# A decoder trunk on one core: the second pair of delta rule heads starts beside the first, two attention heads change places with it, and the embedding results are written from ScalarE

## The chip, the cores and the metric

The kernel runs on one core of a Trainium2 chip. Its time is the device time of one execution in microseconds (us). A core has a matrix engine, TensorE (PE in the rows), and VectorE (DVE), ScalarE (ACT), GpSimd (POOL) and SyncE (SP); each of them works through its own list of instructions strictly in the order in which they were written, and waits where an operand is not there yet. DMA transfers are issued from the queues of SP, POOL or ScalarE.

## The reference

A trunk of two residual layers over 512 positions of width 1024. Layer 0 (even) has two groups of heads that read one input projection: four gated delta rule heads (here a0 to a3, keys and values 128 wide) and four differential attention heads (b0 to b3, two softmax maps of width 64 each). Layer 1 (odd) has eight forgetting attention heads. Each layer ends with a squared-ReLU MLP and with a per-layer embedding that is projected to width 1024 and gated. All of it is float32.

```
# a delta rule head: chunks of 64 positions, then a scan over 8 chunks
kk  = einsum(kb, k) * decay;  a_mat = strict_lower(kk) + eye
sol = triangular_solve(a_mat, [v * beta, kb * exp(gc)])
v_new = u - w @ S;   o = q_dec @ S + qk @ v_new;   S = S * g_last + k_dec^T @ v_new
# a differential head: blocks of 128 queries
a = softmax(mask(q1 k1^T)) - lam * softmax(mask(q2 k2^T));   o = a @ v
# per layer: x += sigmoid(W h) * (p[i] @ w_ple_proj)
```

## The kernel before

Every large matrix is held as a sum of a high and a low part, so that a product takes three matmuls. In the even layer TensorE has two kinds of work. The **fill** is the large projections, which depend on nothing but weights that SP's queue loads into `raw` buffers and ScalarE (`whl`, high part) and VectorE (`whl`, low part) split. The **chains** are the heads: long sequences of short steps, in each of which TensorE waits for another engine.

`even_mixer` is a planner. Its last loop keeps a modelled time, `PE.time`; a chain that is due is moved on by one step, and otherwise the next 128x512 product of the fill is written. The fill comes in the order of one string,

```
ORDER = "a0 a1 w0 v0 v1 b0 b1 a2 a3 w2 b2 b3"
```

where a*h* is the q and k projection of delta head h (48 products of 128x512), w0 and w2 are the values of two delta heads (48 products), v0 and v1 are the values of the differential heads (96 products of 128x256 each), and b*h* is the q and k projection of differential head h (48). Behind the string follow z0 and z1, the output gates of the delta heads, and two passes of `p_proj`: eight transposes of the embedding in a `raw` buffer, two high and low splits of them, then 48 products, whose results ScalarE copies into `pj` and a DMA writes to `p_out` (L343, from SP's queue). A job is written as soon as its condition holds (z0: two delta heads and two differential heads done; z1: all delta heads and three differential heads done; b*h*: head h-2 done). A scheduler afterwards orders the instructions of each engine by when it takes them to be ready.

A delta head (`gdn_head`) runs in two halves. The first, from q and k, makes the decays `et`, the scaled keys `kd`, and with the other head of its pair (0 and 1, 2 and 3) a tile of small triangles. These `small_inverses` copies out to DRAM (`lsc`) and back, broadcast over partitions into `lb` (eight DMAs of POOL's queue, L465); then POOL solves them in 15 dependent steps of a product into `xt` and an addition to `xc` (L471, L473), and builds `x` from them (L560). The second half transposes `x` into `z`, doubles the inverse level by level (`ub`, `yy`), and runs the scan over the chunks (`state`, `vn`, `u`); at its end `rs_t` or `ro` is a reciprocal root on POOL. Heads 2 and 3 begin only when heads 0 and 1 are done (the first line of `gdn_head`, with `ABREAST = 2`).

A differential head (`diff_head`) needs its q and k rotated (`rot`, L727), split into maps in `hl` buffers; then for each block of 128 queries: scores on TensorE (`ax<-hl` and `ax<-kl,hl`), the row maximum on VectorE, the exponential `p` on ScalarE (L920), transposes of `p`, the copy `at` (L937) and the product with the values. Head h begins when head h-1 has begun its last blocks (`started`, at block 1).

The `hl` buffers form one ring of eight tiles. It holds the values of the differential heads (two, all the time), the maps of a head (two), the splits of the embedding (two) and the finished heads (one each).

Of the kernel before, what the change touches and what calls it, by code (L numbers as in the profile page):

```python
# [18 lines left out]
P = 128  # L19
# [49 lines left out]
LAT_A, LAT_B = 1.55, 1.7  # L69
W_G, W_B, W_T, W_V, W_Q = 10.0, 22.5, 20.0, 6.0, 3.6  # L70
Z_B, DSTEP = 3, 3.47
ORDER = "a0 a1 w0 v0 v1 b0 b1 a2 a3 w2 b2 b3"
ABREAST = 2
N_SP = 10
N_ST = 5
SRAW, SWHL, SA = 8, 3, 4
ORDER_MID, ORDER_END = (1, 5, 6, 7, 3, 4, 2), (1, 2, 5, 6, 3, 7, 4)
# [20 lines left out]
def trunk(ctx: ExitStack, tc: tile.TileContext, I, cst, out):  # L98
# [40 lines left out]
    def v3(ap):  # L139
        return ap.rearrange("p (i c) -> p i c", c=P)  # L140
# [182 lines left out]
    def p_proj(layer, stage):  # L323

        pr = tile_of(rawp, F32, "raw")[:, 0:1024].rearrange("p (i c) -> p i c", c=256)
        nc.sync.dma_start(pr, I["p"][layer, 0].rearrange("(i p) c -> p i c", p=P))
        pT = []
        for kt in range(2):
            ps = acc()
            for i in range(NT):  # L330
                PE.transpose(ps[:, i * P:(i + 1) * P], pr[:, i, kt * P:(kt + 1) * P], ident)
            t = hl()
            split(*t, ps)
            pT.append(t)
        yield
        for c in range(2):
            w = wide(I["w_ple_proj"][layer], 0, 512 * c, rawp, whp)
            for i in range(NT):
                ps = acc()
                tok_steps(ps, pT, w, i, slice(0, 512), (0, 1), True, True)  # L340
                y = stage("pj")
                S.activation(out=y, in_=ps, func=AF.Copy)
                nc.sync.dma_start(p_out[layer][i * P:(i + 1) * P, 512 * c:512 * c + 512], y)  # L343
                yield


    def even_mixer(act, first, wba):
        w_in = I["w_in_even"][0]
        with ExitStack() as es:
# [108 lines left out]
            def small_inverses(pair):  # L458

                lc, n = small_l[pair], 2 * NT  # L460
                lsc = dp.tile([P // BASE, BASE * n * BASE], F32, tag="lsc", name="lsc", bufs=1)
                G.dma_start(lsc.rearrange("b (r n) -> b r n", r=BASE), lc.rearrange("p h i c -> p (h i c)"))
                lb = gp.tile([P, BASE, n, BASE], F32, tag="lb", name="lb", bufs=1)
                for a in range(P // BASE):
                    G.dma_start(lb[a * BASE:(a + 1) * BASE].rearrange("p r i c -> p (r i c)"),  # L465
                                lsc[a:a + 1, :].broadcast_to([BASE, BASE * n * BASE]))
                yield 10.0
                xc = small_w[pair].rearrange("p h i c -> p (h i) c")
                tmp = gp.tile([P, n, BASE], F32, tag="xt", name="xt", bufs=1)
                for c in range(BASE - 1, 0, -1):  # L470
                    G.tensor_tensor(out=tmp[:, :, 0:c], in0=lb[:, c, :, 0:c],  # L471
                                      in1=xc[:, :, c].broadcast_to([P, n, c]), op=ALU.mult)
                    G.tensor_tensor(out=xc[:, :, 0:c], in0=xc[:, :, 0:c], in1=tmp[:, :, 0:c], op=ALU.add)  # L473
                yield 10.0
                solved.append(pair)

            def gdn_head(h, qT, kT):
                while len(done) < h + 1 - ABREAST or h >= ABREAST and h not in vts:
                    yield 2.0
                if h >= ABREAST:  # L480
                    yield from decays(h)
                blk = [slice(i * P, (i + 1) * P) for i in range(NT)]
# [5 lines left out]
                pk = aux()  # L488
                for i in range(NT):
                    PE.transpose(pk[:, blk[i]], kT[:, blk[i]], ident)  # L490
                sq, kk = st_("sqk"), gp.tile([P, 2, NT], F32, tag="kk", name="kk", bufs=ABREAST)
                for i in range(NT):
                    S.activation(out=sq[:, blk[i]], in_=pk[:, blk[i]], func=AF.Square, accum_out=kk[:, 0, i:i + 1])
                kd = sp("kd")
                S.activation(out=kd, in_=pk, func=AF.Copy)
                dg = st_("dg")
                V.tensor_tensor(out=v3(dg), in0=v3(pg), in1=mid(gm["minus_base"]), op=ALU.mult)
                second = pair in small_l
# [34 lines left out]
                for i in range(NT):  # L533
                    PE.matmul(pq[:, blk[i]], lhsT=kT[:, blk[i]], rhs=qT[:, blk[i]], start=True, stop=True)
                V.tensor_tensor(out=et, in0=pq, in1=et, op=ALU.mult)
                G.tensor_tensor(out=v3(kd), in0=v3(kd), in1=bc(hcol("ekd", h)), op=ALU.mult)

                pq = aux()
                for i in range(NT):
# [13 lines left out]
                V.tensor_tensor(out=v3(vb), in0=v3(pv), in1=bc(n2), op=ALU.mult)  # L553
                yield 2.0

                while pair not in solved:
                    yield 1.0
                x, xc = sp("x"), small_w[pair][:, sub]
                for i in range(NT):
                    G.tensor_tensor(out=x[:, blk[i]].rearrange("p (b c) -> p b c", c=BASE),  # L560
# [128 lines left out]
            def project_a(h):  # L689
# [11 lines left out]
                    if h < ABREAST:  # L701
                        silu(tiles[-1])
                heads_a.append(tiles[0])
                late.extend(tiles if h >= ABREAST else [])
                spawn(gdn_head(h, *tiles), W_G)

            def values_a(h):
                w = wload(w_in, [(C_V + h * P, 2 * P)])
                for m in range(2):
                    ps = acc()  # L710
                    yield from gemm_steps(ps, w, m, act)
                    late.append(conv_tile(ps, 8 + h + m, "vT"))
                silu(*late)
                for m in range(2):
                    vts[h + m] = late[m - 2], PE.time + W_V * LAT_A
                late.clear()

            def project_b(h):
                c = h * P
# [185 lines left out]
    def diff_head(h, qk, vt, lam, gp, heads, started, done, spawn):  # L905
# [43 lines left out]
        for i in range(NT):  # L949
            yield from values(i, pr[i])  # L950
            if i + 2 < NT:
                pr.append(probs(i + 2))
            if i == 1:
                started.append(h)
            yield DSTEP
        spawn(diff_norm(h, o, gp, heads, done), 1.5, LAT_B)
# [544 lines left out]
```

## Time and profile before

| | us |
|---|---|
| median of 3 runs | 1409.69 (1409.29 to 1410.71) |
| profiled execution | 1409.46, its span 1407.7 |
| TensorE busy | 1379.1 (98%) |
| even layer's mixer, 80 to 325 | 245.0, of it TensorE busy 233.6 |

The mean clock granted to TensorE over the span was 0.995 of full speed. The profile's stretches give for each engine its busy time and the clock; a stretch in which TensorE is neither idle nor below clock 1.00 has nothing to give. The view of waits says for whom TensorE stood still, and the chain of waits goes back from there to the instruction that started late.

### The profile page before, as it was taken

To read this page: it belongs to the slowest core of one execution; us is meant where nothing else is said; L and a number is where in the kernel's file an instruction comes from. 1 tells how busy PE (TensorE), PEld (TensorE's weight loads), DVE (VectorE), ACT (ScalarE), POOL (GpSimd) and SP (SyncE) were. 2 spreads that over 40 slices of the span, in tenths; PEclk is the share of its full clock that TensorE was granted. 3 is DMA by queue.
4 is the path that set the end of the run, shared out by engine and by line. 5 is a ranking of instruction groups with operands and counts; after the bars stand their busy time and mean duration, and the time that the engine had idled before them with its cause. 6 is when DMAs were issued, how large, how long until landed. Compare 5 with 4: busy or idle time off the path is not lost.

```text
span 1407.7 us, 18582 instructions
## 1 busy us (share of the span) xinstructions
PE 1379.1 (98%) x6969; PEld 1146.6 (81%) x6969; DVE 868.3 (62%) x1543; ACT 770.9 (55%) x1302; POOL 178.5 (13%) x241
## 2 busy tenths in 40 slices
PE   8999998999999999999999999999999999999997
PEld 6887876777888888888788888888888888888787
DVE  6847775665555566556856747556646565566675
ACT  6757775764455455554644535535455556455553
POOL 1361054200110110101001000000011020110100
PEclk9999999999999999999999999999999999999999
DMA  6361126126575665748342543661485475765711
GB/s 181 79 116 39 59 80 147 60 87 213 159 172 149 158 155 148 165 136 211 83 97 46 69 95 62 67 84 61 134 245 128 151 168 148 164 148 152 184 54 61
DMA packets 137470, 173.00 MB, mean 123 GB/s; under 512 B 10034, under 2 KB 91524, under 8 KB 137124
## 3 DMA queue, kind: packets, MB, share of 16 engines
q1 hardware_dynamic: 118480, 133.25, 34.9%
q0 software_dynamic: 15936, 35.79, 14.8%
q10 hardware_dynamic: 2964, 2.77, 0.7%
q8 instruction: 55, 0.90, 0.3%
q14 instruction: 35, 0.29, 0.1%
HBM read 156.97 MB, written 6.42 MB: 116 GB/s over the span
## 4 chain that ended last, share of the span: by engine, by line
PE 87%; DVE 5%; ACT 3%; issue 2%; DMA 1%; POOL 1%; POOLq 0%; SPq 0%; ACTq 0%; DVEq 0%
PE mm L90 57%; PE ax L90 26%; PE ax L94 3%; DMA sraw<-w_mlp_down 1%; DVE whl L149 1%; DMA raw<-w_in_even 1%; ACT rot L727 0%; DVE sa L149 0%; DVE swhl L149 0%; DVE x_tok L321 0%; ACT whl L146 0%; ACT L435 0%; POOL rs_t L259 0%; POOL ro L673 0%; ACT swhl L146 0%
## 5 line engine op out<-in xcount | busy, mean ns | idle before, releaser
L90 PE MATMUL mm<-act,whl 128*128 128x512 f32 (+1 forms) x2784 | 653.6, 387 | 0.7 <-ACT act L146 0.5
L90 PEld LDWEIGHTS mm<-act,whl 128*128 128x128 f32 x2784 | 503.1, 188 | 98.9 <-ACT act L146 1.0
L90 PE MATMUL ax<-swhl,sa 128*128 128x512 f32 x1344 | 315.1, 390 | 1.7 <-DVE sa L149 1.6
L90 PEld LDWEIGHTS ax<-swhl,sa 128*128 128x128 f32 x1344 | 251.3, 188 | 56.7 <-DVE sa L149 3.3
L149 DVE TENSOR_TENSOR whl<-raw,whl 128x1024 fp32r<-128x1024 f32 (+1 forms) x139 | 170.5, 1228 | 178.8 <-ACT whl L146 175.3
L149 DVE TENSOR_TENSOR swhl<-sraw,swhl 128x1024 fp32r<-128x1024 f32 x112 | 136.8, 1222 | 119.7 <-ACT swhl L146 119.7
L146 ACT ACTIVATE whl<-raw 128x1024 fp32r<-128x1024 f32 x140 | 148.0, 1057 | 58.4 <-PE mm L90 48.0
L146 ACT ACTIVATE swhl<-sraw 128x1024 fp32r<-128x1024 f32 x112 | 118.7, 1060 | 99.0 <-PE ax L90 80.8
L90 PE MATMUL mm<-whl,act 128*128 128x256 f32 (+2 forms) x720 | 107.3, 306 | 0.2 <-ACT act L146 0.2
L1287 ACT ACTIVATE r<-mm 128x512 f32<-128x512 f32 x64 | 38.2, 596 | 122.7 <-PE mm L90 122.7
L90 PEld LDWEIGHTS mm<-whl,act 128*128 128x128 f32 x720 | 97.3, 190 | 6.6 <-ACT act L146 0.5
L1191 POOL DMA_DIRECT2D sraw<-w_mlp_down x48 | 57.6, 1219 | 250.0 <-DVE swhl L149 103.4
L321 DVE TENSOR_TENSOR x_tok<-x_tok,ax 128x512 f32<-128x512 f32 x114 | 73.7, 681 | 5.6 <-PE ax L90 5.6
L90 PE MATMUL mm<-owhl,act 128*128 128x256 f32 (+1 forms) x336 | 57.9, 329 | 0.0
L90 PE MATMUL mm<-whl,hl 128*128 128x512 f32 x204 | 55.2, 406 | 0.9 <-DVE hl L149 0.8
L90 PE MATMUL mm<-owhl,hl 128*128 128x512 f32 x228 | 54.8, 396 | 0.0
L90 PEld LDWEIGHTS mm<-owhl,act 128*128 128x128 f32 x336 | 49.6, 188 | 6.3
L314 POOL TENSOR_TENSOR rn<-tn,nhalf 128x1 f32<-128x1 f32 x12 | 6.6, 553 | 377.2 <-DVE tn L313 377.2
L1191 POOL DMA_DIRECT2D sraw<-sraw x16 | 14.5, 906 | 300.5 <-DVE swhl L149 275.7
L90 PEld LDWEIGHTS mm<-owhl,hl 128*128 128x128 f32 x228 | 42.4, 188 | 10.1
L1200 ACT ACTIVATE sraw<-sraw 128x1024 f32<-128x1024 f32 x32 | 33.8, 1057 | 26.6 <-DVE swhl L149 15.4
L146 ACT ACTIVATE act<-ax 128x512 fp32r<-128x512 f32 x40 | 22.6, 594 | 43.9 <-PE ax L94 43.9
(341 smaller groups left out, 1596.9 us busy)
## 6 DMA issues: line engine op xcount, KB each, us to landing
raw<-w_mlp_up SPq DMA_DIRECT2D x64, 512.0 KB, 4.2
sraw<-w_mlp_down SPq DMA_DIRECT2D x64, 512.0 KB, 4.5
sraw<-w_mlp_down POOLq DMA_DIRECT2D x48, 512.0 KB, 5.9
raw<-w_in_even SPq DMA_DIRECT2D x32, 256.0 KB, 3.7
sraw<-sraw POOLq DMA_DIRECT2D x16, 512.0 KB, 6.6
raw<-w_ple_gate SPq DMA_DIRECT2D x16, 512.0 KB, 4.5
raw<-w_in_odd SPq DMA_DIRECT2D x16, 512.0 KB, 6.0
raw<-w_in_odd SPq DMA_DIRECT2D x32, 256.0 KB, 6.5
```

The costliest lines, as they stand in the source:

```text
L90: return self.tc.nc.tensor.matmul(out, lhsT=lhsT, rhs=rhs, start=start, stop=stop, skip_group_check=onto)
L94: return self.tc.nc.tensor.transpose(out, in_, ident)
L146: S.activation(out=hi, in_=src, func=AF.Copy)
L149: return (E or V).tensor_tensor(out=lo, in0=src, in1=hi.bitcast(F32), op=ALU.subtract)
L314: G.tensor_tensor(out=r, in0=t, in1=nhalf[:, 0:1], op=ALU.pow)
L321: V.tensor_tensor(out=x_tok[i][:, cs], in0=x_tok[i][:, cs], in1=ps, op=op)
L1191: G.dma_start(o, t, accum_op=ALU.add)
L1200: S.activation(out=t, in_=t, func=AF.Copy, scale=-1.0)
L1287: S.activation(out=r, in_=ps, func=AF.Relu)
```

## The change

The order of the fill is different, heads 2 and 3 no longer wait for heads 0 and 1 before their first half but before `x` is built, and with that some buffers change: `kd` of heads 2 and 3 is made late, from a second transposition of the keys, by one VectorE multiplication in place of a copy on ScalarE and a multiplication on POOL; the triangles come back into two `hl` tiles, by 16 DMAs of half the size, rows 8 to 15 of each triangle first. The heads b1 to b3 may begin at block 0 of the head before, and the results of the embedding products are written from ScalarE's queue.

```diff
-ORDER = "a0 a1 w0 v0 v1 b0 b1 a2 a3 w2 b2 b3"
+ORDER = "a0 a1 w0 v0 b0 a2 a3 b1 w2 v1 b2 b3"
-N_SP = 10
+N_SP = 14
 ...
-                nc.sync.dma_start(p_out[layer][i * P:(i + 1) * P, 512 * c:512 * c + 512], y)
+                nc.scalar.dma_start(p_out[layer][i * P:(i + 1) * P, 512 * c:512 * c + 512], y)
 ...
-                lb = gp.tile([P, BASE, n, BASE], F32, tag="lb", name="lb", bufs=1)
-                for a in range(P // BASE):
-                    G.dma_start(lb[a * BASE:(a + 1) * BASE].rearrange("p r i c -> p (r i c)"),
-                                lsc[a:a + 1, :].broadcast_to([BASE, BASE * n * BASE]))
+                lbs = [hl32().rearrange("p a (r i c) -> p (a r) i c", r=BASE // 4, c=BASE) for _ in range(2)]
+                part = BASE // 2 * n * BASE
+                for j in (1, 0):
+                    for a in range(P // BASE):
+                        G.dma_start(lbs[j][a * BASE:(a + 1) * BASE].rearrange("p r i c -> p (r i c)"),
+                                    lsc[a:a + 1, j * part:(j + 1) * part].broadcast_to([BASE, part]))
 ...
             def gdn_head(h, qT, kT):
-                while len(done) < h + 1 - ABREAST or h >= ABREAST and h not in vts:
-                    yield 2.0
 ...
-                kd = sp("kd")
-                S.activation(out=kd, in_=pk, func=AF.Copy)
+                if h < ABREAST:
+                    kd = sp("kd")
+                    S.activation(out=kd, in_=pk, func=AF.Copy)
 ...
-                while pair not in solved:
+                while pair not in solved or len(done) < h + 1 - ABREAST:
                     yield 1.0
+                if h >= ABREAST:
+                    kd, pk = sp("kd"), aux()
+                    for i in range(NT):
+                        PE.transpose(pk[:, blk[i]], kT[:, blk[i]], ident)
+                    V.tensor_tensor(out=v3(kd), in0=v3(pk), in1=bc(hcol("ekd", h)), op=ALU.mult)
 ...
-                late.extend(tiles if h >= ABREAST else [])
-                spawn(gdn_head(h, *tiles), W_G)
+                if h < ABREAST:
+                    spawn(gdn_head(h, *tiles), W_G)
+                else:
+                    late.append(tiles)
+                if h == HA - 1:
+                    silu(*(t for pair in late for t in pair))
+                    for j, pair in enumerate(late):
+                        spawn(gdn_head(ABREAST + j, *pair), W_G)
 ...
-            if i == 1:
+            if i == 0:
                 started.append(h)
```

Three places of the written order show what that moves. The first is TensorE where the first differential head begins. Before, the values of all heads (`mm<-whl,act`, of v0 and v1) and then b0's 48 and some of b1's products stand ahead of b0's scores (`ax<-hl`):

```order
L90 MATMUL mm<-whl,act 128x256 x42
L94 MATMUL ax<-gen,rope_w 128x128 x8
L90 MATMUL mm<-whl,act 128x256 x66
L90 MATMUL mm<-act,whl 128x512 x79
L90 MATMUL ax_1173<-hl 128x256
L90 MATMUL ax_1173<-kl,hl 128x256
L90 MATMUL mm<-act,whl 128x512
```

In the changed kernel v1 is gone from here, and the products of a2 and a3 stand behind b0's:

```order
L90 MATMUL mm<-whl,act 128x256 x12
L90 MATMUL mm<-act,whl 128x512 x15
L94 MATMUL ax<-gen,rope_w 128x128 x8
L90 MATMUL mm<-act,whl 128x512 x83
L94 MATMUL ax<-gen,x 128x128 x3
L90 MATMUL mm<-act,whl 128x512 x15
L90 MATMUL ax_1089<-hl 128x256
L90 MATMUL ax_1089<-kl,hl 128x256
```

The scores of b0 now come behind 113 products of 128x512, of which the first 48 are b0's own (before 79), and the first transposes of `x` of a delta head, which stood behind these scores, stand ahead of them.

The second place is POOL at the triangles of heads 2 and 3. `ub` of the level doubling and `rs_t` belong to the heads ahead or beside. Before:

```order
L462 DMA lsc<-lc 128x128
L259 TENSOR_TENSOR rs_t<-rs_t,nhalf 128x4
L465 DMA lb<-lsc 16x2048 x8
L583 TENSOR_TENSOR ub<-u,gmask 128x512 x2
L588 TENSOR_TENSOR ub<-u,gmask 128x4x32 x2
L471 TENSOR_TENSOR xt<-lb,xc 128x8x15
L473 TENSOR_TENSOR xc<-xc,xt 128x8x15
```

In the changed kernel the loads go into two tiles of the ring, and the root `ro` of a finished head of the first pair stands ahead of the first solving step:

```order
L462 DMA lsc<-lc 128x128
L467 DMA hl_1746<-lsc 16x1024 x8
L467 DMA hl_1745<-lsc 16x1024 x8
L680 TENSOR_TENSOR ro<-sso,nhalf 128x4
L473 TENSOR_TENSOR xt<-hl_1746,xc 128x8x15
L475 TENSOR_TENSOR xc<-xc,xt 128x8x15
L473 TENSOR_TENSOR xt<-hl_1746,xc 128x8x14
```

The solving of the second pair thus follows the end of a head of the first pair on POOL's list.

The third place is TensorE in the last steps of the differential heads. Before, embedding or gate products (`mm<-whl,hl`) stand between one block's scores and the next:

```order
L90 MATMUL mm<-whl,hl 128x512 x2
L90 MATMUL ax_3004<-hl,at 128x128
L90 MATMUL ax_3007<-hl 128x384
L90 MATMUL ax_3007<-kl,hl 128x384
L90 MATMUL ax_3018<-hl 128x384
L90 MATMUL ax_3018<-kl,hl 128x384
L90 MATMUL mm<-whl,hl 128x512 x2
L94 MATMUL ax_3032<-gen,p_2756 128x128 x4
L90 MATMUL mm<-whl,hl 128x512 x10
```

In the changed kernel:

```order
L90 MATMUL ax_3172<-hl,at 128x128
L90 MATMUL ax_3175<-hl 128x384
L90 MATMUL ax_3175<-kl,hl 128x384
L90 MATMUL ax_3186<-hl 128x384
L90 MATMUL ax_3186<-kl,hl 128x384
L94 MATMUL ax_3259<-gen,p_3032 128x128 x2
L90 MATMUL ax_3264<-hl,at 128x128 x2
L90 MATMUL ax_3268<-hl 128x512
L90 MATMUL ax_3268<-kl,hl 128x512
L90 MATMUL ax_3279<-hl 128x512
L90 MATMUL ax_3279<-kl,hl 128x512
L90 MATMUL mm<-whl,hl 128x512 x48
```

The last two blocks of b3 stand there without any fill between them, and the 48 products of the second embedding pass come behind its last scores.

## Rows read from the trace of the kernel before

**Rows 1.** the page: busy time, share of the span and instructions of each engine

```profile
PE 1379.1 (98%) x6969; PEld 1146.6 (81%) x6969; DVE 868.3 (62%) x1543; ACT 770.9 (55%) x1302; POOL 178.5 (13%) x241
```

**Rows 2.** stretches of the even layer: length, busy by engine, clock, DMA, GB/s

```profile
80.00:120.00 40.00, 38.89 (x212) 32.56 (x211) 22.12 (x46) 24.41 (x44) 19.57 (x40) 0.96 0.45 90
...
160.00:200.00 40.00, 38.25 (x221) 31.60 (x220) 29.81 (x70) 32.85 (x79) 12.60 (x12) 1.00 0.27 83
200.00:240.00 40.00, 34.09 (x154) 25.91 (x153) 25.80 (x61) 23.20 (x57) 16.13 (x26) 0.91 0.58 134
...
280.00:325.00 45.00, 42.59 (x241) 33.80 (x240) 30.80 (x78) 27.57 (x70) 4.45 (x4) 1.00 0.28 92
```

**Rows 3.** PE's waits, 20 to 340: us in total, times, longest

```profile
PE mm L94 <- ACT pj L342: 5.3, 1, 5.3
PE ax L90 <- DVE hl L745: 1.6, 2, 1.1
```

**Rows 4.** a stretch of 2 us inside 200 to 240, columns as rows 2

```profile
226.00:228.00 2.00, 2.00 (x6) 1.22 (x7) 0.39 (x3) 0.00 (x0) 1.08 (x1) 0.50 0.98 252
```

**Rows 5.** chain of waits, 209 to 232: start, us, what

```profile
213.37 7.45 DMA raw<-w_in_even
...
220.90 1.06 ACT whl L146
```

**Rows 6.** POOL in time order, first pair: start, us, count, idle before

```profile
74.22 3.92 POOL L465 DMA_DIRECT2D lb<-lsc  x8
87.90 0.41 POOL L471 TENSOR_TENSOR xt<-lb,xc 128x120 f32<-128x120 f32 x1 [9.77 <-DMA lb<-lsc]
...
104.49 4.46 POOL L560 TENSOR_TENSOR x<-xc,gmask 128x128 f32<-128x128 f32 x8
```

**Rows 7.** POOL in time order, second pair

```profile
176.74 1.03 POOL L673 TENSOR_TENSOR ro<-sso,nhalf 128x4 f32<-128x4 f32 x1 [59.68 <-DVE sso L672]
...
226.92 1.27 POOL L583 TENSOR_TENSOR ub<-u,gmask 128x512 f32<-128x512 f32 x1 [2.58 <-DMA p_out<-pj]
...
235.68 0.41 POOL L471 TENSOR_TENSOR xt<-lb,xc 128x120 f32<-128x120 f32 x1
...
250.96 3.83 POOL L560 TENSOR_TENSOR x<-xc,gmask 128x128 f32<-128x128 f32 x8
```

**Rows 8.** PE in time order: start, us, product, tile, count

```profile
28.28 15.28 PE L90 MATMUL mm<-act,whl 128*128 128x512 f32 x66
...
72.74 5.28 PE L90 MATMUL mm<-whl,act 128*128 128x256 f32 x42
77.86 1.04 PE L94 MATMUL ax<-gen,rope_w 128*128 128x128 f32 x8
...
173.41 0.39 PE L90 MATMUL ax<-state,qT 128*128 128x128 f32 x2
```

**Rows 9.** chain of waits behind b0's k projection, 97 to 107

```profile
98.19 0.59 ACT rot L727
...
101.91 1.18 DVE whl L149
...
104.42 0.68 DVE kl L149
...
105.85 0.67 PE ax L90 x2
```

**Rows 10.** ScalarE by line, 20 to 330: count, busy us, mean ns, idle before

```profile
L920 ACT ACTIVATE p<-ax,mx 128x128 f32<-128x128 f32 (+3 forms) x32 | 16.8, 526 | 8.1 <-DVE mx L917 7.3 <-PE ax L94 0.4
...
L937 ACT ACTIVATE at<-ax 128x128 f32<-128x128 f32 (+3 forms) x16 | 7.0, 440 | 4.1 <-PE ax L94 3.7
L920 ACT ACTIVATION_READ_ACCUMULATOR p<-ax,mx 128x1 f32 x32 | 6.3, 197 | 0.0
```

**Rows 11.** ScalarE in time order around a Silu of the gate

```profile
306.77 1.28 ACT L758 ACT_TABLE_LOAD   x1
308.07 0.60 ACT L758 ACTIVATE zt<-mm 128x512 f32<-128x512 f32 x1
```

More of the change, by code (lines that the diff above doesn't have):

```diff
@@ L470, in small_inverses @@
                 for c in range(BASE - 1, 0, -1):
-                    G.tensor_tensor(out=tmp[:, :, 0:c], in0=lb[:, c, :, 0:c],
+                    G.tensor_tensor(out=tmp[:, :, 0:c], in0=lbs[c // 8][:, c % 8, :, 0:c],
                                       in1=xc[:, :, c].broadcast_to([P, n, c]), op=ALU.mult)
@@ L490, in gdn_head @@
                     PE.transpose(pk[:, blk[i]], kT[:, blk[i]], ident)
-                sq, kk = st_("sqk"), gp.tile([P, 2, NT], F32, tag="kk", name="kk", bufs=ABREAST)
+                sq, kk = st_("sqk"), gp.tile([P, 2, NT], F32, tag="kk", name="kk", bufs=HA)
                 for i in range(NT):
                     S.activation(out=sq[:, blk[i]], in_=pk[:, blk[i]], func=AF.Square, accum_out=kk[:, 0, i:i + 1])
-                kd = sp("kd")
-                S.activation(out=kd, in_=pk, func=AF.Copy)
+                if h < ABREAST:
+                    kd = sp("kd")
+                    S.activation(out=kd, in_=pk, func=AF.Copy)
                 dg = st_("dg")
@@ L535, in gdn_head @@
                 V.tensor_tensor(out=et, in0=pq, in1=et, op=ALU.mult)
-                G.tensor_tensor(out=v3(kd), in0=v3(kd), in1=bc(hcol("ekd", h)), op=ALU.mult)
+                if h < ABREAST:
+                    G.tensor_tensor(out=v3(kd), in0=v3(kd), in1=bc(hcol("ekd", h)), op=ALU.mult)
                 pq = aux()
@@ L703, in project_a @@
                 heads_a.append(tiles[0])
-                late.extend(tiles if h >= ABREAST else [])
-                spawn(gdn_head(h, *tiles), W_G)
+                if h < ABREAST:
+                    spawn(gdn_head(h, *tiles), W_G)
[5 more added lines that the diff above has]
+                        spawn(gdn_head(ABREAST + j, *pair), W_G)
             def values_a(h):
                 w = wload(w_in, [(C_V + h * P, 2 * P)])
+                tiles = []
                 for m in range(2):
@@ L711, in values_a @@
                     yield from gemm_steps(ps, w, m, act)
-                    late.append(conv_tile(ps, 8 + h + m, "vT"))
-                silu(*late)
+                    tiles.append(conv_tile(ps, 8 + h + m, "vT"))
+                silu(*tiles)
                 for m in range(2):
-                    vts[h + m] = late[m - 2], PE.time + W_V * LAT_A
-                late.clear()
+                    vts[h + m] = tiles[m], PE.time + W_V * LAT_A
             def project_b(h):
```

## The prediction

> **What bounds the kernel now.** I read the page first: TensorE is busy for 98% of the span [rows 1], so a gain can only be idle time of TensorE, lost clock, or work taken off it. The stretches show where the even layer has any [rows 2]. Four of them matter here: 80 to 120 has 1.1 us idle and a clock of 0.96, 160 to 200 has 1.75 us idle at full clock, 200 to 240 has 5.9 us idle at 0.91, and 280 to 325 has 2.4 us idle at full clock. A clock of 0.96 over 40 us costs 1.6 us, one of 0.91 costs 3.6 us. Inside 200 to 240 a row of 2 us shows 0.50, the lower of the two levels (1.2 GHz), while TensorE is busy throughout; it follows the long wait [rows 4].
>
> The waits then say for whom TensorE stood [rows 3]: 5.3 us in one piece for `pj`, which frees the accumulator that the transposes of the embedding need, and 1.6 us for b0's rotated maps. The first of these names ScalarE's copy, but the chain of waits goes further back: a load of weights took 7.45 us to come in, and only then could ScalarE do the split for which it stood, with the `pj` copy behind it [rows 5]. The load ran while POOL's eight triangle broadcasts of the second pair were under way, as the DMA column of the same time (0.58 against 0.27 to 0.45 in the other three) lets one expect [rows 2].
>
> **The change part by part.** All fill keeps its amount; a 128x512 product costs 15.28 / 66 = 0.2315 us, a 128x256 one 5.28 / 42 = 0.126 us [rows 8].
>
> Gains. (a) b0's wait goes: 65 products of other heads, 15 us, now lie between its k projection and its scores, where 31 lay, 7.2 us. The chain there takes 105.85 - 98.19 = 7.7 us [rows 9], so 1.1 us of wait and the 1.6 us of clock go. (b) In 200 to 240 the triangles' solving and the embedding products no longer meet: the second pair's triangles are now copied ahead of v1, far ahead of the embedding products, so that the late load loses its neighbour. 5.9 + 3.6 = 9.5 us. (c) v1's 96 products now fill the end of the first pair's scan, 1.75 us idle in 160 to 200. Sum 14.0 us. The 2.4 us of 280 to 325 I leave standing: b3's end is still there.
>
> That `p_out` is written from ScalarE I cost at nothing. TensorE's wait for `pj` came from a load that arrived late, not from the issue of the write, so the queue does not touch its cause [rows 3, 5]. The Trainium skill, in "Trainium Kernel Development and Optimization" (Key Constraints), says that DMAs from all queues run on the same 16 engines and that issuing from several engines saves only the time of issue; by that the move is worth nothing either, and no row here shows the move itself. If ScalarE's issues are not hidden, 16 of them stand behind copies in a queue that is busy 58% of 200 to 240 [rows 2]; the most that they could add is within (L4) below.
>
> Costs. (L0) Heads 2 and 3 transpose their keys again: eight more transposes on TensorE. Eight of them took 1.04 us [rows 8]: 1.0 us. The `kd` work moves from ScalarE and POOL to VectorE, of which each has room.
>
> (L1) First pair's `x`. From 72.74, the start of the 128x256 run, TensorE has 12 of these (1.5), 15 + 83 products of 128x512 (22.7) and eight transposes (0.8) ahead of the transposes of `x`: it is there at 97.7. POOL issues 16 DMAs from 74.22, at 3.92 / 8 = 0.49 us each until 82.1, then solves in 104.49 - 87.90 = 16.6 us and builds three blocks of `x` in 3 x 4.46 / 8 = 1.7 us [rows 6]: 100.4. The wait is 2.7 us. It is 1.2 us if the solving takes the 250.96 - 235.68 = 15.3 us of the second pair [rows 7], and 8.5 us if the triangles land as late as before (start at 87.90). I take 2.7. Behind this wait stand the scores of b0, but no fill can pass.
>
> (L2) Second pair's `x`. POOL's list has the root `ro` of a finished first head ahead of the first solving step, and a chain from TensorE's last `state,qT` product to that root took 176.74 - 173.41 = 3.3 us [rows 7, 8]. Then come `ro` 1.0, the solving 15.3 with, in between, a second root, `rs_t` and three `ub` (1.0, 1.0, 2.5, 0.9), and half of `x`, 1.9: 26.9 us. TensorE meanwhile has 39 products of 128x256 (4.9), 40 of 128x512 (9.3), four scores (1.7) and some 43 small ones (about 4.5): 20.4 us. The wait is 6.5 us; 7.8 with the first pair's 16.6; 1.1 if the five foreign instructions find their time in gaps. I take 6.5, since POOL's list is strict.
>
> (L3) Between b2's k projection and b2's first scores TensorE has only eight transposes of the embedding, eight of `z`, eight small products and two of the embedding, about 3.0 us. The chain of b0 took 7.7 us there, 1.2 of it a weight's split [rows 9]; without that 6.5, and its durations alone, four rotations at 0.59 and four operations of VectorE and ScalarE at 0.6 to 0.7, make 5.0. So 3.5, from 2.0 to 4.7.
>
> (L4) The end of b3. The ring of eight is full there: values 2, maps of b3 2, finished b0 and b1 2, gated a-heads 2. The splits of the second embedding pass have to wait until b3's last scores free the maps, and so its 48 products, all the fill that is left, stand behind them. From b3's second block to its third, ScalarE has two exponentials with their accumulators at 0.53 + 0.20 [rows 10], two loads of the activation table at 1.28 and a Silu between at 0.60 [rows 11], `at` copies, one of 0.60 and the others at 0.3 to 0.44 [rows 10], a weight split at 1.06 [rows 5] and some smaller: 8.9 us, against 6.1 us of TensorE work. That is 2.8 us of wait. After it comes a serial piece: `at` 0.44, an exponential 0.72, two splits 0.63 each, one remainder 0.68: 3.1 us. Together 6.0. The lower end is the serial piece, 3.1; the upper end adds the two other table loads of this stretch, 8.5.
>
> (L5) Clock. A wait like that of 200 to 240 cost 3.6 us of clock behind it, a short one 1.6 [rows 2]. One of the large kind, 3.6, is what I take, from 0 to both and a second large one, 8.4 (rounded down from 8.8).
>
> Sum: 1.0 + 2.7 + 6.5 + 3.5 + 6.0 + 3.6 = 23.3; less 14.0: **+9.3 us**. The profiled execution took 1409.5 (1.8 more than its span), the median is 1409.7, so they stand for each other: 1418.8 us.
>
> **The rivals.** *The late load again.* The triangles, now 16 smaller DMAs, meet another weight load; ScalarE, strict in its order, stands again, and the 9.5 us of (b) are not had: 1418.8 + 9.5 = 1428.3 us. For it: 7.45 us for one load beside eight DMAs [rows 5]. Against it: it took one such meeting out of two, and the first pair's triangles cost no wait on TensorE.
>
> *The written order fits.* The scheduler put each of TensorE's instructions where it expects the operand; if the chains keep that pace, all four waits come out at their low ends at once: 1.0 + 1.2 + 1.1 + 2.0 + 3.1 + 0 - 14.0 = -5.6, that is 1403.9 us. It decides where L1 to L5 together stay below 10.2 us, for then the kernel is faster by over 2.8. For it: before, the same scheduling left TensorE 98% busy, and most of what it lost has one DMA as its root [rows 1, 5]. Against it: b0's 1.6 us shows that a chain can be later than the order expects [rows 3], and POOL and the ring bind whatever it expects.
>
> *Between them.* If only L2 and the clock come out low (1.1 and 0), the sum is 1.0 + 2.7 + 1.1 + 3.5 + 6.0 - 14.0 = +0.3: 1409.8 us, no change.
>
> *Dearer table loads.* In the trace a load of the table takes 1.28 us, and the Silu starts 0.02 us behind it [rows 11]. If a load in the crowded end also made ScalarE empty its queue first, for about as long as the load itself, three of them would make L4 3.8 us longer: 1422.6 us. Against it stands that row. "ScalarE: Activation LUTs" of the Trainium skill (What ACT_TABLE_LOAD costs) has such a drain, of about 1.38 us beside a load of 1.28; by that figure it would be 4.1 us and an estimate of 1422.9.
>
> **How the numbers follow.** What one measurement of this kernel can tell from no change is 0.2%, 2.8 us. My forecast has a chance of 0.47, the late load 0.10, dearer tables 0.05; these three are slower, 0.62 together. The order that fits has 0.28, faster. The case between has 0.10. The forecast's own range, with two of its terms at an end, is 1412 to 1427. The whole range reaches down to the faster case, 1403, and up past the late load, to 1431; all costs at their upper ends would give 1.0 + 8.5 + 7.8 + 4.7 + 8.5 + 8.4 - 14.0 = +24.9, which I leave out.
>
> **What would show it.** In the changed profile, waits of TensorE for `x` at two places (for the first pair around 98, for the second 100 us later), for `hl` of b2, and for `p` or `at` in b3's last blocks, each of 2 to 7 us; TensorE's list without the wait for `pj` of 5.3 us; full clock in 80 to 120. The forecast is wrong if the even layer ends earlier than before: then either POOL starts its second solving well ahead of TensorE (no wait for `x`), or the split of the embedding comes into the ring before b3 ends. A `raw` load of over 7 us with ScalarE waiting for it would speak for the late load.

## The result and the profile after

The changed kernel takes 1431.74 us (1428.67 to 1432.89, 5 runs) against 1409.29 for the kernel before (1408.00 to 1410.71, 5 runs): 1.0155 times as long, interval 1.0144 to 1.0166. The direction was forecast, but +9.3 us and at most 1431 were too little for +22.4. The profiled execution has a span of 1429.9 us, 22.2 more than before, and all of it is in the even layer's mixer: the second half of its output projection (`mm<-owhl,hl`) begins at 355.74, before at 333.55.

The page of the changed kernel, engine line: eight matmul instructions more than in [rows 1], and 10 us more busy time.

```profile
PE 1389.4 (97%) x6977; PEld 1155.5 (81%) x6977; DVE 871.9 (61%) x1545; ACT 767.5 (54%) x1296; POOL 180.1 (13%) x255
```

The four stretches of [rows 2] in the changed kernel (third column TensorE busy, then the other engines; the third figure from the end is the clock):

```profile
80.00:120.00 40.00, 34.77 (x135) 26.56 (x133) 19.82 (x37) 19.10 (x32) 17.05 (x44) 0.87 0.35 85
160.00:200.00 40.00, 39.94 (x268) 35.21 (x268) 28.93 (x89) 23.97 (x71) 17.26 (x31) 1.00 0.28 82
200.00:240.00 40.00, 32.70 (x213) 26.58 (x212) 28.47 (x59) 23.81 (x51) 19.13 (x38) 0.88 0.19 54
280.00:325.00 45.00, 38.12 (x156) 28.52 (x157) 26.08 (x73) 28.41 (x62) 4.17 (x3) 0.81 0.26 88
```

Only 160 to 200 got better. The waits of TensorE between 20 and 360 us (total, times, longest) replace those of [rows 3], of which none is left (the name behind the arrow is the last thing that the profile saw TensorE wait for):

```profile
PE ax L90 <- ACT at L950: 6.8, 4, 4.8
PE mm L90 <- DVE qT L429: 3.2, 1, 3.2
PE ax L94 <- DVE mx L930: 3.0, 1, 3.0
PE mm L90 <- ACT hl L146: 2.4, 1, 2.4
PE mm L90 <- ACT whl L146: 1.5, 1, 1.5
...
PE ax L90 <- ACT x L630: 1.1, 1, 1.1
```

Behind the longer of them the clock falls to its lower level (1.2 GHz). Stretches of 2 us, columns as above:

```profile
88.00:90.00 2.00, 2.00 (x7) 1.54 (x6) 0.00 (x0) 0.00 (x0) 1.69 (x5) 0.50 0.00 0
92.00:94.00 2.00, 2.00 (x10) 1.66 (x9) 0.00 (x0) 0.93 (x1) 1.61 (x6) 1.00 0.00 0
236.00:238.00 2.00, 2.00 (x6) 1.33 (x7) 1.17 (x5) 0.00 (x0) 0.00 (x0) 0.50 0.33 115
...
306.00:308.00 2.00, 1.35 (x5) 1.14 (x5) 1.28 (x8) 1.04 (x4) 0.88 (x1) 0.50 0.00 0
312.00:314.00 2.00, 2.00 (x6) 1.53 (x5) 1.97 (x5) 0.60 (x1) 0.00 (x0) 0.50 0.00 0
316.00:318.00 2.00, 2.00 (x11) 1.63 (x10) 0.65 (x2) 1.88 (x5) 0.00 (x0) 1.00 0.36 133
```

At 88 and at 312 TensorE is never idle and still does 6 or 7 products where it does 10 or 11 at 92 and 316. So a wait can cost twice: its own length, and the slow stretch behind it. In TensorE's time order (start, us, products, in brackets the idle time) the end of b3 shows both, the waits at 299 to 307 and the fill, which begins only behind the last scores:

```profile
293.59 0.60 PE L94 MATMUL ax<-gen,p 128*128 128x128 f32 x4
299.03 2.08 PE L90 MATMUL ax<-hl,at 128*128 128x128 f32 x8 [4.84 <-ACT at L950]
...
301.75 0.79 PE L90 MATMUL ax<-hl,at 128*128 128x128 f32 x2 [0.43 <-ACT at L950]
...
306.65 1.22 PE L90 MATMUL ax<-hl,at 128*128 128x128 f32 x4 [1.32 <-ACT at L950]
...
310.43 13.60 PE L90 MATMUL mm<-whl,hl 128*128 128x512 f32 x48
```

For all runs I made the same account, from windows of 2 us between 20 us and the start of `mm<-owhl,hl`. Idle is length minus TensorE's busy time; slowed is the sum of (1 - clock) times busy time; the rest is the start of `mm<-owhl,hl` less both. One profiled execution each; the medians are of all timed runs. Where the profiled execution lay off its median (e2 3.6 us above it, e18 2.4 above, e10 3.1 below, e11 2.0 below), the account is that of this execution.

| run | median | `owhl` starts | idle | slowed | rest |
|---|---|---|---|---|---|
| before | 1409.3 | 333.6 | 13.4 | 4.8 | 315.4 |
| changed | 1431.7 | 355.7 | 24.4 | 16.4 | 314.9 |
| e1_pout_sync | 1431.6 | 355.3 | 25.0 | 14.0 | 316.4 |
| e2_zb2 | 1429.3 | 355.3 | 22.5 | 16.6 | 316.2 |
| e3_wt18 | 1415.9 | 339.1 | 17.5 | 5.0 | 316.6 |
| e4_spin | 1430.9 | 356.2 | 18.9 | 9.2 | 328.0 |
| e5_spin2 | 1429.0 | 352.4 | 20.8 | 11.1 | 320.5 |
| e6_order_on_before | 1416.5 | 339.8 | 16.7 | 6.1 | 317.0 |
| e7_old_order | 1441.7 | 366.1 | 23.9 | 24.9 | 317.3 |
| e8_wt18_solve_dve | 1415.7 | 337.7 | 14.4 | 3.0 | 320.2 |
| e9_spin_all | 1428.8 | 353.4 | 17.6 | 8.0 | 327.8 |
| e10_started_on_before | 1427.8 | 347.7 | 17.3 | 14.7 | 315.7 |
| e11_pout_on_before | 1407.1 | 329.0 | 12.1 | 0.0 | 316.9 |
| e12_early_pair_on_before | 1425.2 | 348.8 | 24.3 | 8.4 | 316.1 |
| e13_pt_outside_ring | 1428.5 | 350.2 | 22.4 | 10.9 | 316.9 |
| e14_pt_and_solve | 1423.3 | 345.2 | 21.1 | 4.9 | 319.2 |
| e15_early_pair_pt_outside | 1414.0 | 336.9 | 15.9 | 3.3 | 317.7 |
| e16_before_pout_pt | 1407.4 | 332.6 | 12.5 | 2.9 | 317.1 |
| e17_pt_and_exp_gate | 1427.6 | 346.5 | 22.6 | 7.8 | 316.1 |
| e18_before_pout_exp_gate | 1410.4 | 335.3 | 12.2 | 6.6 | 316.5 |

The rest is 315 to 318 us in most runs, 320 to 328 with added products (e4, e5, e9), and 319 and 320 in e14 and e8, which solve the second pair's triangles on VectorE; why these two are higher was not traced. From before to after it did not grow, so idle and slowed time hold the whole change: idle grew by 11.0 us and slowed by 11.6. How it divides between the two is known to some 2 or 3 us only: e1, which takes as long as the changed kernel, has 25.0 and 14.0.

### The profile page after: what moved, and what is told of

It is laid out like the page before. It is cut to its first block, busy times and chain, and to the rows that moved or that the text cites. A ratio compares the mean times of both kernels' runs of the same rounds, so it can differ in the third digit from the quotient of the medians.

```text
span 1429.9 us, 18591 instructions
## 1 busy us (share of the span) xinstructions
PE 1389.4 (97%) x6977; PEld 1155.5 (81%) x6977; DVE 871.9 (61%) x1545; ACT 767.5 (54%) x1296; POOL 180.1 (13%) x255
## 4 chain that ended last, share of the span: by engine, by line
PE 88%; DVE 4%; ACT 3%; POOL 1%; issue 1%; DMA 1%; POOLq 0%; ACTq 0%
PE mm L90 59%; PE ax L90 26%; PE ax L94 3%; DMA sraw<-w_mlp_down 1%; ACT rot L740 0%; DVE whl L149 0%; ACT hl L146 0%; DVE swhl L149 0%; DVE sa L149 0%; POOL x L567 0%; DVE x_tok L321 0%; ACT swhl L146 0%; POOL xc L475 0%; POOL xt L473 0%; ACT whl L146 0%
## 5 line engine op out<-in xcount | busy, mean ns | idle before, releaser
L90 PE MATMUL mm<-whl,act 128*128 128x256 f32 (+2 forms) x720 | 110.4, 308 | 0.2 <-ACT act L146 0.2
L90 PEld LDWEIGHTS mm<-whl,hl 128*128 128x128 f32 x204 | 40.5, 203 | 11.6 <-ACT hl L146 3.0
L1213 ACT ACTIVATE sraw<-sraw 128x1024 f32<-128x1024 f32 x32 | 33.8, 1057 | 24.9 <-DVE swhl L149 15.3
```

The costliest lines, as they stand in the source:

```text
L90: return self.tc.nc.tensor.matmul(out, lhsT=lhsT, rhs=rhs, start=start, stop=stop, skip_group_check=onto)
L1213: S.activation(out=t, in_=t, func=AF.Copy, scale=-1.0)
```

## The experiments

All are compared with runs of the kernel before on the same chip (medians 1408.56 to 1409.84). Each edit also lets the scheduler order the engines' lists anew, so a difference is that of the edit with its new order.

**Which part of the change costs.** Each part alone, on the kernel before or with the old order.

```diff
 # e6_order_on_before: the kernel before with
+ORDER = "a0 a1 w0 v0 b0 a2 a3 b1 w2 v1 b2 b3"
 # e10_started_on_before: the kernel before with
-            if i == 1:
+            if i == 0:
 # e11_pout_on_before: the kernel before with
-                nc.sync.dma_start(p_out[layer]...
+                nc.scalar.dma_start(p_out[layer]...
 # e7_old_order: the changed kernel with
+ORDER = "a0 a1 w0 v0 v1 b0 b1 a2 a3 w2 b2 b3"
 # e12_early_pair_on_before: e7_old_order with
+            if i == 1:
 # e1_pout_sync: the changed kernel with nc.sync.dma_start(p_out[layer]...
```

e6_order_on_before: 

> The kernel before with the new order of the fill alone; heads 2 and 3 still begin when heads 0 and 1 are done. Theory (the order of the fill takes the cover from the places where TensorE then waits): slower than before by 6 to 25 us, 1416 to 1435 us, with waits in the stretch behind 280 us and half clock there. Rival (the early first half of heads 2 and 3 on POOL and the triangles in the ring make the loss, not the order): within 3 us of before, 1407 to 1413 us.

e7_old_order: 

> The changed kernel with the old order of the fill; all its other parts stay. Theory: b3's last blocks have fill between them again and keep full clock, most of the 22 us go: 1408 to 1416 us. Rival (POOL's list, in which the roots of the first pair and the solving of the second stand in each other's way, makes the loss): 1422 us or more.

e10_started_on_before: 

> The kernel before with one part of the change alone: a differential head may begin at block 0 of the head before. Theory (with the old order and the late second pair there is fill between the blocks): within 4 us of before, 1406 to 1414 us. Rival (the heads b that overlap more are what uses the fill up before the end): slower by 6 us or more, 1416 us and above.

e12_early_pair_on_before: 

> The changed kernel with the old order of the fill and with the old start of the differential heads: of the change the early first half of heads 2 and 3 is left, with its buffers, and the queue of the embedding results. Theory (the early first half is the part that with the old order costs 32 us, since its small steps use the fill's cover early and the triangles fill POOL's list and the ring): 1430 to 1445 us. Rival (the differential heads that overlap more make the most of it): 1410 to 1420 us.

The order alone costs 6.7 us (1416.53 against 1409.84; ratio 1.0034 to 1.0064), the early second pair on the old order, with its buffers and ScalarE's queue, 16.5 us (1425.20 against 1408.70; 1.0097 to 1.0131), between its theory and its rival, the earlier start of the b heads 19.1 us (1427.83; 1.0114 to 1.0148), and both of the latter with the old order 31.9 us (1441.74 against 1409.84; 1.0212 to 1.0242). So in e7 and e10 the theory failed, and in e6 its size held but its place was wrong (a wait of 6.4 us for `x`, and not one behind 280). With the new order the start of the b heads does nothing: their projections come too late for it, and with block 1 in its place all five engines get the same instructions in the same order. What is left to act in the changed kernel is the order and the early pair, 6.7 + 16.5 = 23.2, against 22.4 together. That they add up may be chance: on the old order the early pair and the earlier start do not (16.5 and 19.1, together 31.9), and the waits are others. In e12 TensorE stood at other places than in the changed kernel, where the embedding's splits were late (columns as above):

```profile
232.27 1.22 PE L90 MATMUL mm<-whl,hl 128*128 128x512 f32 x2 [6.88 <-ACT hl L146]
245.43 1.09 PE L94 MATMUL ax<-gen,do 128*128 128x128 f32 x4 [6.30 <-DVE do L981]
```

e1_pout_sync: 

> The changed kernel with the embedding results written from SyncE's queue again, nothing else. Theory (waits of TensorE at four places, and the lower clock behind each of them, make the 22 us; the queue of these writes is no part of it): within 2 us of the changed kernel, 1430 to 1434 us. Rival (the writes stand on ScalarE among the copies for which TensorE waits in the last blocks of b3): 5 us or more faster than the changed kernel, below 1427 us.

e11_pout_on_before: 

> The kernel before with the embedding results written from ScalarE's queue. Theory (the wait of 5.3 us for a result's copy had a late load behind it, not the queue): the wait stays, within 2 us of before, 1408 to 1412 us. Rival (SyncE's queue, in which the writes stood among the loads, made the load late): the 5.3 us and the clock behind them go, 1400 to 1405 us.

In the changed kernel the queue is worth nothing: 1431.62. On the kernel before it gave 1.6 us (ratio 0.9978 to 0.9997), just inside the theory's range by time. But the theory's mechanism failed: the wait of 5.3 us for `pj` did not stay. In e11 it is 0.7 us in two pieces (e16 and e18, which have the same edit, show the same two):

```profile
212.77 3.03 PE L90 MATMUL mm<-whl,hl 128*128 128x512 f32 x12 [0.37 <-ACT pj L342]
216.14 1.66 PE L90 MATMUL mm<-whl,hl 128*128 128x512 f32 x6 [0.34 <-ACT pj L342]
```

SyncE issued the first of the loads there at 206.9 us, not at 212.6. Waits for the embedding's splits came in place of a part of it, and all idle time fell by 1.3 us only. Whether the queue did this by itself is not shown, since the lists of all five engines come out in another order. The profiled execution of e11, the fastest of its ten, had full clock in 200 to 240; that of e16 had 0.91 there. These two were the fastest kernels of the study, e11 with that interval just faster than the kernel before.

**What the low clock costs.** Products that nothing uses keep TensorE busy where it waited.

```diff
             po = aux2()
+            spin = vt[0][:, h * P:(h + 1) * P].bitcast(F32)
+            for _ in range(SPIN.get((h, i), 0)):   # e5_spin2: {(2, 3): 18, (3, 0): 1, (3, 1): 4}
+                nc.tensor.matmul(po[:, 0:P], lhsT=spin, rhs=spin, start=True, stop=True)
```

e5_spin2: 

> The run with extra products of no use again, with half as many (18, 1 and 4, each of two passes of 0.115 us: 5.3 us in all), so that they end before ScalarE's copies arrive, where the 52 ran 5 us beyond them. Theory (the low clock behind the waits costs time of its own): the waits keep their length, nothing from 293 to 325 us runs at half clock, 4 to 7 us faster than the changed kernel, 1425 to 1428 us. Rival (the low clock is hidden by the waits): within 2 us of the changed kernel, 1430 to 1434 us.

e9_spin_all: 

> The changed kernel with extra products of no use at three of its four waiting places: 14 where TensorE waited 3.0 us at 206, 8 where it waited 2.4 us at 232, and 18, 1 and 4 in the last blocks of b2 and b3; each is two passes of 0.115 us. No other work is taken out or moved on purpose. Theory (the low clock behind the waits costs time of its own; over 200 to 330 us it lengthened the busy time by 12 us): 6 to 10 us faster than the changed kernel, 1422 to 1426 us, with a clock of 1.00 from 200 us on. Rival (the chains of the other engines set the end, and TensorE's pace between the waits is hidden): within 3 us, 1429 to 1435 us.

e5 came out at 1429.01 (2.7 us faster than the changed kernel, between the two numbers), e9 at 1428.82 (2.9 us faster, where its theory gave 6 to 10: there the rival holds). Against the kernel before the ratios are 1.0120 to 1.0150 and 1.0122 to 1.0152, which overlap the changed kernel's 1.0144 to 1.0166, so these gains are at the edge of what the runs can tell. In e5's profile 5.3 us of added products brought the slowed time down by 5.3 us (1.1 of them in 80 to 120, where the edit does nothing) and the idle time by 3.6, and `owhl` began 3.4 us earlier. A first run with 52 of them (e4_spin) had full clock from 280 us to the end of the mixer, but the products ran some 5 us in all past the waits: 1430.85, between its theory (1425 to 1428) and its rival (1431 to 1436). In e9, 10.3 us of products took 8.4 us off the slowed time, 6.8 off the idle time, and 2.4 off the end. So slowed time that goes comes back only in part: TensorE is then sooner at the next thing that is late, and idle and slowed time are not independent of each other.

The timed runs show the cost without added products: within most kernels, the runs with the lower mean clock are the longer ones. Of e18's twelve the two shortest took 1408.3 us at a mean clock of 0.998, the longest 1415.9 at 0.991; e13's four go from 1424.5 at 0.992 to 1432.0 at 0.986. In e1 (0.8 us apart at 0.984 to 0.988) it can't be seen. Over the 98 timed runs of the changed kernel and the experiments, compared within each kernel, 0.001 of mean clock goes with some 0.9 us, where 0.001 of the span would be 1.4. This is a correlation, and what lowers the clock in one execution and not in the next is open.

**What makes the waits.** One cause at a time.

```diff
 # e2_zb2: the second gate projection may come when two b heads are done
-Z_B, DSTEP = 3, 3.47
+Z_B, DSTEP = 2, 3.47
 # e3_wt18: the rotary tables are due earlier
-W_G, W_B, W_T, W_V, W_Q = 10.0, 22.5, 20.0, 6.0, 3.6
+W_G, W_B, W_T, W_V, W_Q = 10.0, 22.5, 18.0, 6.0, 3.6
 # e8_wt18_solve_dve, e14_pt_and_solve: solving on VectorE for the second pair
+                    E = V if pair else G
 # e13_pt_outside_ring, and with e12: e15; with e11: e16
-            t = hl()
+            t = own() if own else hl()      # own: two tiles of the "qkv" buffers, second pass
 # e17_pt_and_exp_gate (on e13), e18 (on e11)
-                    S.activation(out=zt[m], in_=pz[m], func=AF.Silu)
+                    S.activation(out=zt[m], in_=pz[m], func=AF.Exp, scale=-1.0)
+                    (VectorE: add 1, reciprocal, times pz[m])
```

e2_zb2: 

> The changed kernel with one number different: the second gate projection may be written when two differential heads are done, not three, so that its 48 products stand among b3's last steps, where TensorE waited 6.6 us and ran at half clock for 16 us. Theory: these waits go, and the clock stays up there, 8 to 13 us faster than the changed kernel, 1419 to 1424 us. Rival (the fill that is used here is then missing behind b3, where the last copies and norms have no cover): at most 3 us faster, 1429 us or more.

e13_pt_outside_ring: 

> The changed kernel with the two splits of the second embedding pass in buffers of the convolutions (free by then) instead of the ring of eight. TensorE's list is the same up to b3's second block; from there the 48 products stand among b3's steps, and the 48 of the second gate projection behind them. Theory (the full ring keeps this fill out of b3's last blocks, which is where 6.6 us of waits and 7.3 us of slower work lie): 9 to 14 us faster than the changed kernel, 1418 to 1423 us, full clock from 290 us on. Rival (as with the second gate projection, the fill only changes places and the waits come behind it): at most 4 us faster, 1427 us or more.

e17_pt_and_exp_gate: 

> The run with the second embedding pass's splits outside the ring, and in it the gate's Silu made of an exponential on ScalarE and an addition, a reciprocal and a product on VectorE, so that ScalarE needs no other activation table there. Theory (the wait of 4.85 us at 294 us that stayed is ScalarE's list, of which two table loads are 2.56 us): the wait falls to 2.5 us or less, with less half clock behind it, 3 to 6 us faster than that run (1428.5), 1422 to 1426 us. Rival (another entry of the list, or VectorE's three added steps, holds the copies as long): within 2 us, 1427 to 1431 us.

All three rivals hold: 1429.25, 1428.50 and 1427.62, 2.5 to 4.1 us faster than the changed kernel (ratios to the kernel before 1.0130 to 1.0163, 1.0117 to 1.0159 and 1.0118 to 1.0144; the first two overlap the changed kernel's). In each the wait was cured where it was, and came back beside it. With the ring freed, the fill itself waited first, since its operands come out of the same list of ScalarE:

```profile
298.77 5.74 PE L90 MATMUL mm<-whl,pT 128*128 128x512 f32 x12 [4.85 <-ACT pT L146]
```

The chain of waits of the changed kernel has that list (start, us, what):

```profile
293.62 0.58 ACT qT L686
...
294.21 1.28 ACT L771
...
295.50 0.60 ACT zt L771
...
296.12 0.76 ACT L933
...
297.41 0.56 ACT p L933 x2
297.98 0.52 ACT hl L146
298.49 0.49 ACT at L950
...
299.03 2.09 PE ax L90 x8
```

L771 at 294.21 and L933 at 296.12 are the two table loads around the Silu. Without them (e17) the one wait of 4.85 became four of 1.07, 0.49, 1.87 and 1.25 us, the latter two for VectorE, which has the gate's new steps ahead of `pT`'s second part:

```profile
290.40 0.49 PE L90 MATMUL ax<-hl,at 128*128 128x128 f32 x2 [1.07 <-ACT at L956]
292.59 0.49 PE L90 MATMUL ax<-hl,at 128*128 128x128 f32 x2 [0.49 <-ACT at L956]
296.24 0.73 PE L90 MATMUL mm<-whl,pT 128*128 128x512 f32 x2 [1.87 <-DVE zt L774]
298.44 13.67 PE L90 MATMUL mm<-whl,pT 128*128 128x512 f32 x46 [1.25 <-DVE pT L149]
```

This is no clean test of the table loads: for the two of 1.28 us that the wait had, VectorE got two reciprocals of 128x512, and one of them takes 3.35 us there, against 0.68 for a product of the same size.

e3_wt18: 

> The changed kernel with one number different: the rotary tables are due a little earlier, so that b0's projection is written before a2's instead of into the middle of it. Theory: the wait of 3.2 us for an accumulator at 81 us and the half clock behind it (some 3 us) go, and of these 6 us 1 to 2 come back as a wait for x, which POOL has only at 100: 4 to 5 us faster than the changed kernel, 1427 to 1428 us. Rival (POOL's solving is the bound of this stretch, whatever stands before it): within 2 us of the changed kernel.

15.9 us, four times what the theory gave, and for another reason: the wait for an accumulator stayed (2.9 us, now for the copy of v0), but the planner, with b0 earlier, wrote the second embedding pass's transposes at 247 us, not at 292.7, so that its 48 products were ready in b3's last blocks. TensorE had 43.23 us of 45 busy there, at full clock. The edit moved other work too, so this is one arrangement that covers b3's end, not a measurement of one cause. (Transposes of the changed kernel and of e3, then e3's stretch.)

```profile
292.71 1.04 PE L94 MATMUL mm<-gen,raw 128*128 128x128 f32 x8
...
247.06 1.03 PE L94 MATMUL mm<-gen,raw 128*128 128x128 f32 x8
...
280.00:325.00 45.00, 43.23 (x207) 33.57 (x206) 29.90 (x76) 31.99 (x65) 3.02 (x3) 1.00 0.31 107
```

e15_early_pair_pt_outside: 

> The run with the early second pair on the old order (1425.2 us), with the second embedding pass's splits outside the ring. Theory (the triangles' two tiles in the ring are why the splits came 6.9 us late at 232 us, and the 6.3 us at 245 us follow from it): 6 to 12 us faster, 1413 to 1419 us. Rival (a late load of weights, 5.4 us in the chain there, and ScalarE's order make these waits): within 3 us, 1422 to 1428 us.

1414.0 (1.0024 to 1.0054 of before), 11 us faster than e12, as the theory said: there, where the splits were late at 232, more room for them is most of the loss. On the kernel before it changed nothing (e16_before_pout_pt: 1407.43 against e11's 1407.10), as expected of it: 

> The kernel before with the embedding results written from ScalarE (1407.1 us against 1408.7) and the second embedding pass's splits outside the ring. Theory (before, the ring doesn't bind, so nothing changes): within 2 us of 1407 us. Rival (it binds there too, at the embedding products at 221 us): 1402 to 1404 us, faster than both kernels.

 And the gate without table loads (e18_before_pout_exp_gate) came out at 1410.36, 2 to 3 us above e11 and outside both ranges: where fill covers them, taking the loads away gains nothing. Whether the three steps of VectorE, with 13.4 us of reciprocals in all, make the 2 to 3 us is not shown.

e14_pt_and_solve: 

> The run before this one in the list, and also the second pair's 15 solving steps on VectorE. Theory (the waits at 206 us come from POOL's strict list, those at the end from the ring, and they add): 2 to 5 us faster than with the splits outside the ring alone, 1414 to 1420 us. Rival (VectorE's added steps cost as much as POOL's order): no faster than that run.

1423.34, 5.2 us faster than e13, where 2 to 5 were expected; the 1414 to 1420 us that went with it took e13's own theory for granted and were missed. In the profile the wait for `u`, the end of the first pair's second head, all but went with the solving gone from POOL's list (the root and the wait in the changed kernel, then the wait in e14):

```profile
206.71 1.01 POOL ro L680
...
208.58 0.66 PE L94 MATMUL ax<-gen,u 128*128 128x128 f32 x4 [3.05 <-DVE mx L930]
...
203.32 0.66 PE L94 MATMUL ax<-gen,u 128*128 128x128 f32 x4 [0.64 <-DVE u L682]
```

The stretch of 200 to 245 shows 2.0 us less idle and 1.2 less slowed time; 3.2 us are slowed time of 80 to 125, where the edit does nothing. On e3 the same edit gave 0.1 us (e8_wt18_solve_dve, 1415.73): 

> The run with the earlier rotary tables (1415.9 us), and in it the 15 solving steps of the second pair on VectorE instead of POOL, so that they don't stand between POOL's roots. Theory (TensorE's waits of 1.3 and 3.6 us at 202 and 209 us come from POOL's strict list, and the half clock behind them costs 3 us): both waits and the clock loss go, 4 to 8 us faster than that run, 1408 to 1412 us, level with the kernel before or a little faster. Rival (VectorE, which all chains need there, becomes late by the 30 added instructions): 1415 us or more.

 Whether POOL's list costs more than the 2 us is not settled.

## Why the prediction was wrong, step by step

The step that failed is (L5), the clock. It took one slow stretch of 3.6 us where the changed kernel has 16.4 us of slowed time, and let the 5.2 us of before go (4.8 by the account above): -1.6 in the sum. Measured are +11.6 us, or +9.2 in e1. The trace of before had shown both of its waits followed by a slow stretch (1.1 us of wait by 1.6, 5.3 by 3.6 us), and I had four waits of 2.7 to 6.5 us on paper; one price for each, by those rows, would have been the consistent reading, and at the end of b3, where wait follows wait, the clock stayed low for 16 us. By e9 and the runs within one kernel a part of this slowed time would have come out as idle time at full clock, so the two terms can't be told apart to the last us.

The waits themselves, 18.7 us less 8.8 us that went, made +9.9; measured is +11.0 us of idle. That these agree is in part luck, for it is a sum of right and wrong places:

- (a) b0's wait went, but by luck. Of the 113 products ahead of b0's scores the first 24 are a2's q projection, not b0's own, so 32 and not 65 lie behind b0's k projection (31 before). What made the room is that TensorE itself waited 2.0 us for two weight splits just there; b0's last operand was ready at 111.3 us, and TensorE came at 112.3 (rows below). That b0's clock loss would go with it was wrong.
- (b) The wait for `pj` went, and (c), 1.75 us in 160 to 200, too [rows 2, 3]. But that the queue of `p_out` does not touch the wait for `pj`, for which the prediction put it at nothing, does not stand: e11 has 0.7 us of it on the kernel before. At nothing it came out in the changed kernel, where the wait is gone with either queue (e1).
- (L0) eight more transposes: 6977 against 6969 products.
- (L1) 2.7 us for `x` of the first pair: none. POOL held its part (three blocks of `x` by 99.9 us, forecast 100.4), but TensorE came at 106.2, not at 97.7: late by those splits, by the low clock behind 84, and by a wait I had not seen, 3.2 us at 81. There a2's q projection is written ahead of b0's (the rotary tables are not due yet), and by the written order all three accumulators are then held until ScalarE and VectorE have done a2's convolution and v0's copies, which stand behind it in ScalarE's list. Why they stand there is open.
- (L2) 6.5 us for `x` of the second pair: 0.6 at `gen,x`. 3.0 us stood ahead of it at `gen,u`, for the second root `ro`, which POOL did at 206.7 us in the midst of the solving. That POOL's strict list makes a wait was right (e14), the place and the size were not.
- (L3) 3.5 us: 1.1 and 2.4, right in place and size. What TensorE stood for were not b2's maps but two operands that ScalarE's list had between and behind the same rotations: `x` of a delta head (230.4) and the embedding's split (233.8).
- (L4) 6.0 us (5.9 by its own terms): 4.84 + 0.43 + 1.32 = 6.6, right in size and place, with the table loads in the chain of waits as named. The cures that follow from the naming, one at a time, brought 2.5 to 4 us. In e3, where the fill's operands were ready long before, idle and slowed time from 280 us to the end are 2.8 and 0 against 7.9 and 7.3, some 12 us less; that the ring alone stood against it in the changed kernel is not shown, since e13 freed it.

The rows of (a) and (L1), TensorE from 84 to 112 us:

```profile
84.67 19.45 PE L90 MATMUL mm<-act,whl 128*128 128x512 f32 x72 [3.22 <-DVE qT L429]
105.61 0.73 PE L90 MATMUL mm<-act,whl 128*128 128x512 f32 x2 [1.48 <-ACT whl L146]
106.18 0.49 PE L94 MATMUL ax<-gen,x 128*128 128x128 f32 x3
107.20 5.30 PE L90 MATMUL mm<-act,whl 128*128 128x512 f32 x15 [0.53 <-DVE whl L149]
112.33 0.28 PE L90 MATMUL ax<-hl 128*128 128x256 f32 x1
```

Of the rivals, the late load did not come in the changed kernel: the weight loads between 168 and 240 us landed within 4.9 us. The drain beside a table load, for which the prediction named "ScalarE: Activation LUTs" of the Trainium skill (What ACT_TABLE_LOAD costs), is not in the trace: the copy before the load ends at 294.20, the load starts at 294.21 and ends at 295.49, and the Silu starts at 295.50.

## What to carry to other kernels

Where a kernel lives on fill between chains, price a new wait of the matrix engine as its length plus a slow stretch behind it, taken from a stretch after a wait in the same trace, and add stretches where waits come close together. Read the sum as an upper figure: with 8.4 us of slowed time gone, e9 was 2.9 us faster. Before moving a chain earlier, look for the fill that it leaves for the last chain, and whether that fill's operands will be ready by then: its buffers and its place in the other engines' lists decide that. Curing the last link of such a place moved the wait to the next one in e2, e13 and e17. And a row that names a late load does not say why it was late: here the load came earlier when writes left its queue and all lists were ordered anew.

## What was not expected of the hardware

The clock behind the same wait is not the same each time. Nine profiled executions have the wait of 3.2 us at 81 (the changed kernel, e1, e2, e4, e5, e9, e13, e14, e17). The slowed time between 80 and 120 us was 4.4 us in the changed kernel, 1.5 in e1 and none in e14 and e17, where the clock stood at 1.00 all through; the others lie between 3.2 and 4.7 (e1 first, then e17):

```profile
80.00:120.00 40.00, 34.70 (x154) 26.88 (x152) 22.22 (x43) 21.32 (x36) 17.41 (x44) 0.96 0.36 85
```

```profile
80.00:120.00 40.00, 34.06 (x158) 26.55 (x158) 23.91 (x45) 22.90 (x37) 19.54 (x45) 1.00 0.36 83
```

So the price of a wait in one trace is one draw of several. The scatter of a kernel's timed runs, 7.5 us in e13 and 7.6 in e18, goes with the mean clock of the single run, as shown above.
